# SSD decays in a hybrid trunk kernel: running sums sent through a DRAM scratch instead of selected inputs and matmuls

## The chip, the cores and the metric

The kernel runs on one core of one Trainium2 chip. The core has five engines that work side by side and wait for one another through semaphores. TensorE (PE in the profile) multiplies matrices, and its weight loads are listed apart as PEld. VectorE (DVE) does elementwise work, ScalarE (ACT) activations and copies, GpSimd (POOL) more elementwise work and selects, SyncE (SP) issues the DMA transfers. A DMA queue is worked off by sixteen DMA engines. SBUF is the working memory, PSUM holds what TensorE writes, DRAM is the large memory outside.

The metric is the device time of one execution in microseconds (us), lower is better. Three timed runs of the kernel before gave 1427.46, 1426.99 and 1427.30 us, median 1427.3.

## The reference

The reference is a trunk of two layers over 512 tokens of width 1024. Layer 0 is a Mamba-2 (SSD) mixer followed by a squared-ReLU MLP, layer 1 a stick-breaking attention followed by another MLP. A LayerNorm of `alpha * h + sublayer(h)` stands after each of the four. The change touches only the SSD mixer, and in it the decays:

```
a_cs      = cumsum(a)                                   # a = dt * -exp(a_log), per head
decay_mat = exp(segsum(a))                              # exp(a_cs[l] - a_cs[s]) for s <= l, else 0
cb        = einsum("bclgn,bcsgn->bcgls", cc, bc)        # C_l . B_s, one per group
y_diag    = einsum("bcgls,bcgrls,bcsgrp->bclgrp", cb, decay_mat, xc)
states    = einsum("bclgn,bcgrl,bclgrp->bcgrpn", bc, exp(a_cs[-1] - a_cs), xc)
prev      = scan: carry * exp(a_cs[-1]) + states        # from chunk to chunk
y_off     = einsum("bclgn,bcgrpn,bcgrl->bclgrp", cc, prev, exp(a_cs))
y         = rmsnorm_per_group((y_diag + y_off + D * x) * silu(z)) * norm_w @ w_out
```

There are 32 heads in 8 groups of 4. The sums over a chunk don't depend on where chunks are cut, and the kernel uses four chunks of 128 tokens where the reference uses eight of 64.

## The kernel before

Products are made in split precision: each operand is a rounded part (`hi`, `h`) plus a remainder (`lo`, `l`), and `mm3` (L206) issues three matmuls for one product. A weight tile is fetched by `emit_w` (L149): SP loads `wr`, ACT casts it to `wh` (L190), DVE or, for every fourth tile, POOL subtracts to get `wl` (L192). There are two buffers for `wr` and four for `wh`/`wl`, so SP waits for an older tile's split before it fetches the next.

`ssm` (L565) is the SSD layer. It loads the transposed input `xf` in five pieces, splits it into `x_h` and `x_l`, and then runs:

- `time_steps` (L617): the time-step projection `pdt` (24 matmuls), a transpose `pdtt`, a chain of some twenty small operations on 128x128 tiles for the softplus (L628 to L640), `da` (L644) and its split `da_h`, `da_l` (L645, L646). Then four small matmuls make the running sums `pa` (tile `pacs`) with the triangle `tri_le`, and the totals `pt_` (tile `ptot`) with ones. From these come `E`, `bdec` and `dec_s`.
- for each group g: `in_bc` and `in_x` (projections `pB`, `pC`, `px`, convolution and SiLU), `in_z` (`pz`), `in_xt` (transposes `pxt`, the tiles `xd`, `xe`, `dx`), `decays`, `scores` (C.B into `cbm`), and for each chunk c `front` (the product of decay and score, split into `W`, and the state carry `prev`) and `back` (`po`, `py`). Then `gate` and `finish` (`pyt`). After groups 3 and 7 `tok_out` multiplies by the output weights (`so`).

`decays(q)` (L762) makes the decay tiles of a group before. For each of the four chunks POOL copies `da_h` and `da_l` of four heads over 128 columns with the triangle cut out (two affine_selects of 128x512, tiles `dm`, one buffer each), PE multiplies both by `tri_gt` into a PSUM tile `sg` (two matmuls of 128x512), and ACT takes one exponential of 128x512 into `dec`. The upper triangle of `dec` is 1 there, and the select on `cbm` (L788) puts zeros in. In `front`, `dec` is multiplied by `cbm` on DVE, and on POOL for chunk 3.

What sets the order: a scheduler with a timeline model places each engine's instructions when the program is built; each engine then works through its own list strictly in order. Tiles of one tag share a fixed number of buffers. PSUM has two tags of four buffers, `mm` (`pdt`, `pB`, `pC`, `px`, `pz`, `so`) and `bg` (the small tiles and `sg`). `table_order` (L661) keeps the SiLUs and the exponentials of ACT in batches, since changing between them costs a table load.

Of the kernel before, what the change touches and what calls it, by code (L numbers as in the profile page):

```python
# [11 lines left out]
F32 = mybir.dt.float32  # L12
F32R = mybir.dt.float32r
AF = mybir.ActivationFunctionType
ALU = mybir.AluOpType
# [20 lines left out]
def trunk(ctx: ExitStack, tc: tile.TileContext, io):  # L36
# [6 lines left out]
    ps = ctx.enter_context(tc.tile_pool(name="ps", bufs=4, space=PSUM))  # L43

# [9 lines left out]
    def f(x):  # L54
        return x.bitcast(F32)
# [11 lines left out]
    for _ in range(14):  # L67
# [497 lines left out]
    def ssm(sp, nxt_ln):  # L565
# [38 lines left out]
        def small(name, dt=F32):  # L604
            return sp.tile(CH, dt, name=name)
# [9 lines left out]
        dec_s = small("dec_s")  # L615

        def time_steps():  # L617
# [31 lines left out]
            for o, l in ((pa, tri_le), (pt_, ones_r)):  # L649
                nc.tensor.matmul(o, l, da_h, start=True, stop=False)  # L650
                nc.tensor.matmul(o, l, da_l, start=False, stop=True)
            nc.scalar.activation(E, pa, AF.Exp)
# [109 lines left out]
        def decays(q, cs=range(NT)):  # L762
            g = q.g
            hs = slice(4 * g, 4 * g + 4)
            if cs[0] == 0:
                q.dec = []
            for c in cs:
                nm = f"{g}_{c}"
                dm = pair(f"dm{nm}", S4, "dm", 1)
                for o, i in zip(dm, (da_h, da_l)):  # L770
                    nc.gpsimd.affine_select(o, f(i[:, c, hs]).unsqueeze(2).to_broadcast(S4), pattern=[[0, 4], [1, P]],
                                            compare_op=ALU.is_ge, fill=0.0, base=0, channel_multiplier=-1)
                pseg = psum("bg", S4, f"sg{nm}")
                nc.tensor.matmul(pseg, tri_gt, dm[0], start=True, stop=False)
                nc.tensor.matmul(pseg, tri_gt, dm[1], start=False, stop=True)
                dec = sp.tile(S4, F32, tag="dec", name=f"dec{nm}", bufs=4)
                table_order("exp", nc.scalar.activation(dec, pseg, AF.Exp))
                q.dec.append(dec)

        def scores(q):  # L780
            g = q.g
            pcb = psum("bg", [P, NT, P], f"cb{g}")
            for c in range(NT):
                cs = slice(c * P, (c + 1) * P)
                mm3(pcb[:, c, :], (q.B[0][:, cs], q.B[1][:, cs]), (q.C[0][:, cs], q.C[1][:, cs]), True, True)
            q.cbm = sp.tile([P, NT, P], F32, tag="cbm", name=f"cbm{g}", bufs=1)
            nc.scalar.copy(q.cbm, pcb)
            nc.gpsimd.affine_select(q.cbm, q.cbm, pattern=[[0, NT], [1, P]], compare_op=ALU.is_ge, fill=0.0,  # L788
                                    base=0, channel_multiplier=-1)
            q.pr = [None] * NT  # L790
            q.W = [None] * NT

        def front(q, c):
# [4 lines left out]
            eng = nc.gpsimd if c == 3 else nc.vector  # L798
            eng.tensor_tensor(dec, dec, q.cbm[:, c, :].unsqueeze(1).to_broadcast(S4), op=ALU.mult)
# [81 lines left out]
        run(in_x(cur, 1))  # L881
        decays(cur)
        in_xt(cur)
        v = None
        for g in range(G):
# [15 lines left out]
            front(q, 1)  # L901
# [3 lines left out]
            front(q, 2)  # L905
# [3 lines left out]
            front(q, 3)  # L909
# [22 lines left out]
            if g % 4 == 3:  # L932
# [5 lines left out]
                else:  # L938
                    nxt_ln.load_rows(lambda j, c0: sp.tile(S4, F32, tag="dec", name=f"lnr{j}{c0}", bufs=4)
# [340 lines left out]
```

## Time and profile before

| | before |
|---|---|
| median of three timed runs | 1427.3 us |
| profiled execution, its own time | 1426.79 us |
| span of that execution | 1424.7 us |
| mean granted TensorE clock | 0.994 |
| busy, share of the span: PE / PEld | 98% / 84% |
| busy: DVE / ACT / POOL | 76% / 55% / 16% |
| moved by DMA | 162.99 MB, mean 114 GB/s |

Busy time of PE counts matmuls from start to a modelled end, and one starts before the one ahead has ended. What a matmul costs a full PE is therefore the distance from its start to the next start, not its own duration. Granted clock is the share of TensorE's full clock that the hardware allowed in a stretch. The SSD layer is the first 450 us or so of the span; the two MLPs and the attention follow.

### The profile page before, as it was taken

What the parts mean: (1) busy time and instruction counts of PE and PEld (TensorE: products, weight loads), DVE (VectorE), ACT (ScalarE), POOL (GpSimd) and SP (SyncE); (2) the same over time, 40 slices, a digit from 0 to 9 for tenths busy, and PEclk for the clock granted to TensorE, in tenths of its full rate; (3) what the DMA queues carried; (4) which work ended last, traced back from release to release, by engine and by line L of the source; (5) the groups of instructions that cost most, each with busy time, mean ns of one, the idle gap of its engine ahead of it and who ended that gap; (6) DMA issues with size and microseconds to landing.
All of it is one profiled execution on the core that took longest, in us unless ns stands there. A gap on an engine that the chain in (4) does not pass through costs nothing. (4 is left out here: it accounts for less than half of the span.)

```text
span 1424.7 us, 19323 instructions
## 1 busy us (share of the span) xinstructions
PE 1394.1 (98%) x7414; PEld 1199.9 (84%) x7414; DVE 1078.2 (76%) x1530; ACT 783.9 (55%) x1264; POOL 221.4 (16%) x249
## 2 busy tenths in 40 slices
PE   9999999999999999999999899999999999999996
PEld 6898897889997988888888789899878888888885
DVE  5798898368877695876849868787867876858587
ACT  5556574246653453626345468898842735454453
POOL 2344555135443100000000200000000000000001
PEclk9999999999999999999999999999999999999999
DMA  5223212221223356455443421121223455454533
GB/s 185 75 77 131 75 60 75 89 89 60 75 75 104 125 157 179 132 179 161 148 148 120 146 89 38 52 75 45 89 75 118 131 165 162 149 175 136 176 111 126
DMA packets 46699, 162.99 MB, mean 114 GB/s; under 512 B 5520, under 2 KB 5776, under 8 KB 46608
## 3 DMA queue, kind: packets, MB, share of 16 engines
q1 hardware_dynamic: 44016, 157.44, 35.4%
q10 hardware_dynamic: 2592, 4.33, 1.0%
q8 instruction: 58, 0.95, 0.3%
q14 instruction: 33, 0.27, 0.1%
HBM read 159.65 MB, written 2.10 MB: 114 GB/s over the span
## 5 line engine op out<-in xcount | busy, mean ns | idle before, releaser
L190 ACT CAST wh<-wr 128x1024 fp32r<-128x1024 f32 x235 | 246.7, 1050 | 328.5 <-DMA wr<-w 165.1
L192 DVE TENSOR_TENSOR wl<-wr,wh 128x1024 fp32r<-128x1024 f32 x218 | 268.4, 1232 | 184.3 <-ACT wh L190 182.9
L208 PE MATMUL f<-ln_hl,wh 128*128 128x512 f32 (+1 forms) x544 | 201.2, 371 | 0.0
L209 PE MATMUL f<-ln_hh,wl 128*128 128x512 f32 (+1 forms) x544 | 201.1, 370 | 0.0
L207 PE MATMUL f<-ln_hh,wh 128*128 128x512 f32 (+1 forms) x544 | 200.4, 371 | 0.0
L208 PEld LDWEIGHTS f<-ln_hl,wh 128*128 128x128 f32 x544 | 102.3, 188 | 17.6 <-DVE ln_hl L399 0.2
L209 PEld LDWEIGHTS f<-ln_hh,wl 128*128 128x128 f32 x544 | 102.3, 188 | 17.4
L207 PEld LDWEIGHTS f<-ln_hh,wh 128*128 128x128 f32 x544 | 101.9, 188 | 17.5
L347 POOL TENSOR_TENSOR ln_rs<-ln_sums 128x1 f32<-128x1 f32 (+1 forms) x6 | 3.1, 523 | 635.3 <-ACT lnr L345 635.3
L208 PE MATMUL X<-wl,hP 128*128 128x512 f32 x192 | 74.7, 389 | 0.0
L207 PE MATMUL X<-wh,hP 128*128 128x512 f32 x192 | 74.7, 389 | 0.0
L209 PE MATMUL X<-wh,l 128*128 128x512 f32 x192 | 74.2, 390 | 0.2 <-DVE l L460 0.2
L209 PE MATMUL pz<-wh,x_l 128*128 128x256 f32 x256 | 72.8, 284 | 0.0
L208 PE MATMUL pz<-wl,x_h 128*128 128x256 f32 x256 | 72.6, 284 | 0.0
L207 PE MATMUL pz<-wh,x_h 128*128 128x256 f32 x256 | 72.5, 283 | 0.0
L459 ACT CAST hP<-r 128x512 fp32r<-128x512 f32 x80 | 48.1, 620 | 32.4 <-DVE r L471 31.5
L192 POOL TENSOR_TENSOR wl<-wr,wh 128x1024 fp32r<-128x1024 f32 x17 | 42.5, 2503 | 93.3 <-ACT wh L190 92.9
L207 PE MATMUL px<-x_h,wh 128*128 128x512 f32 x128 | 50.8, 397 | 0.0
L208 PE MATMUL px<-x_l,wh 128*128 128x512 f32 x128 | 50.2, 393 | 0.0
L209 PE MATMUL px<-x_h,wl 128*128 128x512 f32 x128 | 50.2, 392 | 0.0
L208 PE MATMUL Y<-wl,hP 128*128 128x512 f32 x128 | 49.8, 389 | 0.0
L208 PEld LDWEIGHTS pz<-wl,x_h 128*128 128x128 f32 x256 | 48.7, 190 | 0.9
(1365 smaller groups left out, 3930.7 us busy)
## 6 DMA issues: line engine op xcount, KB each, us to landing
wr<-w SPq DMA_DIRECT2D x160, 512.0 KB, 3.6
wr<-w_bc SPq DMA_DIRECT2D x16, 512.0 KB, 3.6
wr<-w_x SPq DMA_DIRECT2D x16, 512.0 KB, 3.6
wr<-w_z SPq DMA_DIRECT2D x16, 512.0 KB, 3.5
wr<-w_so SPq DMA_DIRECT2D x16, 512.0 KB, 3.6
rawa<-w SPq DMA_DIRECT2D x16, 512.0 KB, 3.6
rawc<-w SPq DMA_DIRECT2D x16, 512.0 KB, 4.5
wr<-w_qk SPq DMA_DIRECT2D x16, 512.0 KB, 3.6
```

Source lines behind the costliest of these rows:

```text
L190: nc.scalar.copy(hi, raw)
L192: eng.tensor_sub(lo, raw, f(hi))
L207: nc.tensor.matmul(out, a[0], b[0], start=start, stop=False, skip_group_check=skip)
L208: nc.tensor.matmul(out, a[0], b[1], start=False, stop=False, skip_group_check=skip)
L209: return nc.tensor.matmul(out, a[1], b[0], start=False, stop=stop, skip_group_check=skip)
L347: nc.gpsimd.tensor_add(rs, self.sq[:, t0:t1, 0], self.sq[:, t0:t1, 1])
L459: nc.scalar.copy(h, src)
```

## The change

The decay of a chunk is exp(a_cs[l] - a_cs[s]) for s <= l. The tile has s on the partitions and l along the columns. After the change a_cs[l] is brought to all 128 partitions by DMA, and a_cs[s], which is one number per partition, enters as the bias of the exponential:

- `time_steps` makes the running sums a second time, transposed (`pcsr`, two matmuls of 128x128, a PSUM tile of tag `mm`), copies them to SBUF (`csr`) and writes them to a DRAM tile `cs_rows`; a scaled copy of `pa` gives the negative sums `ncs`.
- `spread(q, c)` loads the four rows of a group and chunk from DRAM to all partitions (256 KB, queue of SP) and puts -1e30 above the diagonal with one affine_select in place on POOL. The four spreads of a group are called in `front` of the group ahead, one per chunk. `dec` has six buffers instead of four.
- `decays(q)` is 16 exponentials of 128x128 with a bias each, in place.
- the `dm` selects, the `sg` matmuls, `tri_gt` and the select on `cbm` are gone; `front` multiplies on DVE for every chunk.

```diff
+    dp = ctx.enter_context(tc.tile_pool(name="dp", bufs=1, space=bass.MemoryType.DRAM))
...
-    tri_gt = cp.tile([P, P], F32R, name="tri_gt")
-    nc.gpsimd.affine_select(tri_gt, one, pattern=[[-1, P]], compare_op=ALU.is_gt, fill=0.0,
-                            base=0, channel_multiplier=1)
...
+        ncs = small("ncs")
+        cs_rows = dp.tile([NT, H, P], F32, name="cs_rows")
...
             for o, l in ((pa, tri_le), (pt_, ones_r)):
                 nc.tensor.matmul(o, l, da_h, start=True, stop=False)
                 nc.tensor.matmul(o, l, da_l, start=False, stop=True)
+            pr = psum("mm", [P, P], "pcsr")
+            for i, x in enumerate((da_h, da_l)):
+                nc.tensor.matmul(pr, x.rearrange("p c h -> p (c h)"), tri_le, start=i == 0, stop=i == 1)
+            rows = sp.tile([P, P], F32, name="csr")
+            nc.scalar.copy(rows, pr)
+            nc.sync.dma_start(cs_rows.rearrange("c h t -> (c h) t"), rows)
+            nc.scalar.activation(ncs, pa, AF.Copy, scale=-1.0)
...
-        def decays(q, cs=range(NT)):
+        def spread(q, c):
             g = q.g
-            hs = slice(4 * g, 4 * g + 4)
-            if cs[0] == 0:
+            if c == 0:
                 q.dec = []
-            for c in cs:
-                nm = f"{g}_{c}"
-                dm = pair(f"dm{nm}", S4, "dm", 1)
-                for o, i in zip(dm, (da_h, da_l)):
-                    nc.gpsimd.affine_select(o, f(i[:, c, hs]).unsqueeze(2).to_broadcast(S4), pattern=[[0, 4], [1, P]],
-                                            compare_op=ALU.is_ge, fill=0.0, base=0, channel_multiplier=-1)
-                pseg = psum("bg", S4, f"sg{nm}")
-                nc.tensor.matmul(pseg, tri_gt, dm[0], start=True, stop=False)
-                nc.tensor.matmul(pseg, tri_gt, dm[1], start=False, stop=True)
-                dec = sp.tile(S4, F32, tag="dec", name=f"dec{nm}", bufs=4)
-                table_order("exp", nc.scalar.activation(dec, pseg, AF.Exp))
-                q.dec.append(dec)
+            dec = sp.tile(S4, F32, tag="dec", name=f"dec{g}_{c}", bufs=6)
+            nc.sync.dma_start(dec.rearrange("p h t -> p (h t)"),
+                              cs_rows[c, 4 * g:4 * g + 4, :].rearrange("h t -> (h t)").partition_broadcast(P))
+            nc.gpsimd.affine_select(dec, dec, pattern=[[0, 4], [1, P]], compare_op=ALU.is_ge, fill=-1e30,
+                                    base=0, channel_multiplier=-1)
+            q.dec.append(dec)
+
+        def decays(q):
+            for c, dec in enumerate(q.dec):
+                for h in range(4):
+                    i = 4 * q.g + h
+                    table_order("exp", nc.scalar.activation(dec[:, h, :], dec[:, h, :], AF.Exp,
+                                                            bias=ncs[:, c, i:i + 1]))
...
             nc.scalar.copy(q.cbm, pcb)
-            nc.gpsimd.affine_select(q.cbm, q.cbm, pattern=[[0, NT], [1, P]], compare_op=ALU.is_ge, fill=0.0,
-                                    base=0, channel_multiplier=-1)
...
-            eng = nc.gpsimd if c == 3 else nc.vector
-            eng.tensor_tensor(dec, dec, q.cbm[:, c, :].unsqueeze(1).to_broadcast(S4), op=ALU.mult)
+            nc.vector.tensor_tensor(dec, dec, q.cbm[:, c, :].unsqueeze(1).to_broadcast(S4), op=ALU.mult)
...
         run(in_x(cur, 1))
+        for c in range(NT):
+            spread(cur, c)
         decays(cur)
...
+            def first(c):
+                front(q, c)
+                if nxt:
+                    spread(nxt, c)
+
             scores(q)
             fill.run(4)
-            front(q, 0)
+            first(0)
```

(The other three calls of `front` become `first` in the same way.)

The scheduler places the work anew. First place, the start of the program on PE. `pdt` is the time-step projection, `pB` the first projection of group 0, `pacs`, `ptot` and `pcsr` the running sums, totals and transposed sums. Before, right behind the warm-up:

```order
L207 MATMUL pdt<-x_h,wdthi 128x512
L208 MATMUL pdt<-x_l,wdthi 128x512
L209 MATMUL pdt<-x_h,wdtlo 128x512
L207 MATMUL pB_241<-x_h,wh_129 128x512
L208 MATMUL pB_241<-x_l,wh_129 128x512
L207 MATMUL pdt<-x_h,wdthi 128x512
L209 MATMUL pB_241<-x_h,wl_130 128x512
L207 MATMUL pB_241<-x_h,wh_129 128x512
```

After the change, the end of the 24 `pdt` matmuls, which now stand together, and what follows:

```order
L207 MATMUL pdt<-x_h,wdtlo 128x512
L625 MATMUL pdtt<-ident,dT 128x128 x4
L650 MATMUL pacs<-da_h,tri_le 128x128
L650 MATMUL ptot<-da_h,ones_r 128x128
L654 MATMUL pcsr<-tri_le,da_h 128x128
L205 MATMUL pB_250<-x_h,wh_129 128x512
L206 MATMUL pB_250<-x_l,wh_129 128x512
```

Before, `pB` was woven into `pdt`, `pC` and `px` stood next, and `pacs` came far behind, after the 24 matmuls each of `pB`, `pC` and of the next group's `pB`, 48 of `px` and 23 of the next `pC`. Now no `pB` matmul stands ahead of the first `pcsr` matmul, which reads `da_h`. `pcsr` was written as a tile of the same PSUM tag as `pB`, and ahead of it in the program.

Second place, the same stretch on DVE, which makes `da_h` from `pdtt` (`dtt` are its temporaries, `ca_B` and `ca_C` the convolutions, `wl` weight remainders). Before:

```order
L628 TENSOR_TENSOR dtt_201<-pdtt,hv 128x128
L672 SCALAR_TENSOR_TENSOR ca_C_315<-pC_290,cw,ca_C_315 128x509
L694 CAST B0h<-ca_B_266 128x512
L639 TENSOR_SCALAR dtt_201<-dtt_201 128x128
L631 TENSOR_SCALAR dtt_201<-dtt_201 128x128
L695 TENSOR_TENSOR B0l<-ca_B_266,B0h 128x512
L632 RECIPROCAL dtt_201<-dtt_201 128x128
L694 CAST C0h<-ca_C_315 128x512
```

After the change:

```order
L628 TENSOR_TENSOR dtt_203<-pdtt,hv 128x128
L190 TENSOR_TENSOR wl_296<-wr_293,wh_295 128x1024
L639 TENSOR_SCALAR dtt_203<-dtt_203 128x128
L631 TENSOR_SCALAR dtt_203<-dtt_203 128x128
L632 RECIPROCAL dtt_203<-dtt_203 128x128
L633 TENSOR_TENSOR dtt_203<-dtt_203 128x128
L634 TENSOR_TENSOR dtt_203<-dtt_203 128x128
L635 TENSOR_SCALAR dtt_203<-dtt_203 128x128
L637 SCALAR_TENSOR_TENSOR dtt_203<-dtt_203 128x128 x6
L638 SCALAR_TENSOR_TENSOR dtt_203<-dtt_203 128x128
L640 SCALAR_TENSOR_TENSOR dt<-dtt_203 128x128
L644 SCALAR_TENSOR_TENSOR dtt_204<-dt,dtt_204 128x128
```

The chain stands in one piece now, with one weight remainder (of the second `px` weight tile) behind its first step; the convolutions have moved behind it.

Third place, group 1, on POOL and on SP. `pv` is the state carry of group 1, `dec` a spread tile of group 2 or 3, `yg` the output accumulation. POOL before:

```order
L788 AFFINE_SELECT cbm_990<-cbm_990 128x512
L799 TENSOR_TENSOR dec_3_955<-dec_3_955,cbm_990 128x512
L192 TENSOR_TENSOR wl_1359<-wr_1356,wh_1358 128x1024
L810 TENSOR_TENSOR pv_0_1021<-pv_0_1021,bdec 128x256 x2
L841 TENSOR_TENSOR yg_1097<-yl_0_1108,dx_886 128x256
```

POOL after the change:

```order
L190 TENSOR_TENSOR wl_1386<-wr_1383,wh_1385 128x1024
L814 TENSOR_TENSOR pv_0_1028<-pv_0_1028,bdec 128x256
L776 AFFINE_SELECT dec_2_1180<-dec_2_1180 128x512
L814 TENSOR_TENSOR pv_0_1028<-pv_0_1028,bdec 128x256
L776 AFFINE_SELECT dec_3_1263<-dec_3_1263 128x512
L845 TENSOR_TENSOR yg_1114<-yl_0_1125,dx_914 128x256
```

SP after the change, the loads that these selects wait for (before, the same weights stood there without the `dec` rows):

```order
L164 DMA wr_1509<-w_z 128x1024
L947 DMA v<-x 128x4x1024
L164 DMA wr_1578<-w_z 128x1024
L774 DMA dec_2_1180<-cs_rows 128x512
L774 DMA dec_3_1263<-cs_rows 128x512
L164 DMA wr_1656<-w_x 128x1024
```

A select that waits for a load now stands between the two carry multiplies of a group, and that load stands behind a weight load on SP.

More of the change, by code (lines that the diff above doesn't have):

```diff
@@ L904, in ssm @@
             fill.run(4)
-            front(q, 2)
+            first(2)
             fill.run(4)
@@ L908, in ssm @@
             fill.run(4)
-            front(q, 3)
+            first(3)
             fill.run(4)
@@ L938, in ssm @@
                 else:
-                    nxt_ln.load_rows(lambda j, c0: sp.tile(S4, F32, tag="dec", name=f"lnr{j}{c0}", bufs=4)
+                    nxt_ln.load_rows(lambda j, c0: sp.tile(S4, F32, tag="dec", name=f"lnr{j}{c0}", bufs=6)
                                      .rearrange("p a c -> p (a c)"), T)
```

2 lines of the change are left out of this document (1 added, 1 removed).

## The prediction

> **What bounds the kernel now.** I read the page's totals first, then the busy times by stretch, then the waits of PE.
>
> ```profile
> PE 1394.1 (98%) x7414; PEld 1199.9 (84%) x7414; DVE 1078.2 (76%) x1530; ACT 783.9 (55%) x1264; POOL 221.4 (16%) x249
> 50.00:200.00 150.00, 148.06 (x961) 133.99 (x961) 131.88 (x209) 94.00 (x170) 74.85 (x78) 1.00 0.27 87
> 250.00:400.00 150.00, 150.00 (x910) 133.87 (x909) 106.13 (x167) 77.43 (x134) 54.49 (x56) 1.00 0.26 78
> PE pyt L864 <- DVE yg L859: 1.4, 1, 1.4
> PE st L207 <- ACT dec L777: 1.0, 1, 1.0
> ```
>
> In both stretches of the SSD layer (the columns are the stretch and its length, then busy us of PE, PEld, DVE, ACT and POOL) PE is busy for all but 2 of 300 us; DVE has 88% and 71%, ACT 63% and 52%. The last two rows are the two longest waits of PE inside the groups, 2.4 us together, against some 400 us of them. So PE bounds the groups: a matmul removed there shortens them by what it took from the stream, and work put on ACT or DVE costs nothing as long as their gaps hold it.
>
> **What is removed from PE.** The `sg` matmuls are listed in eight groups of eight, 64 in all; first and last group, then two places in the stream:
>
> ```profile
> L774 PE MATMUL sg<-dm_0h,tri_gt x8: 393/476/481, 49.1 to 399.3; 128*128 128x512 f32 x8
> L775 PE MATMUL sg<-dm_3l,tri_gt x8: 389/477/485, 60.4 to 413.1; 128*128 128x512 f32 x8
> ```
>
> ```profile
> 98.26 0.40 PE L774 MATMUL sg<-dm_1h,tri_gt 128*128 128x512 f32 x1
> 98.50 0.28 PE L208 MATMUL pz<-wl,x_h 128*128 128x256 f32 x1
> 98.96 0.40 PE L775 MATMUL sg<-dm_1l,tri_gt 128*128 128x512 f32 x1
> 99.19 0.28 PE L209 MATMUL pz<-wh,x_l 128*128 128x256 f32 x1
> ```
>
> They last 0.39 to 0.48 us but overlap. From start to next start they take 0.24 and 0.23 us. 64 x 0.235 = **15.0 us** leave PE. (By duration it would be some 26 us, which the stream never spent.)
>
> **What is added at the start.** The order of the changed kernel puts all of `pdt`, `pdtt`, `pacs`, `ptot` and the first `pcsr` ahead of the first `pB`. PE works through its list in order, so it now waits for the whole softplus chain with nothing else to do. Before, PE had `px` and more to run while that chain went on, from 29.55 us to the first `pacs` at 48.39. I rebuild the chain from its rows of before:
>
> ```profile
> 14.11 3.91 DVE L590 TENSOR_TENSOR x_l<-xf,x_h 128x512 fp32r<-128x512 f32 x4 [2.95 <-ACT x_h L589]
> 23.43 0.58 ACT L622 COPY dT<-pdt 128x512 f32<-128x512 f32 x1
> 28.41 0.60 PE L625 MATMUL pdtt<-ident,dT 128*128 128x128 f32 x4
> 29.55 0.28 DVE L628 TENSOR_TENSOR dtt<-pdtt,hv 128x128 f32<-128x128 f32 x1
> 9.38 6.63 SPq L166 DMA_DIRECT2D wr<-w_x  x2
> wr<-w_x SPq DMA_DIRECT2D x16, 512.0 KB, 3.6
> 23.91 1.05 ACT L190 CAST wh<-wr 128x1024 fp32r<-128x1024 f32 x1
> 25.00 1.22 DVE L192 TENSOR_TENSOR wl<-wr,wh 128x1024 fp32r<-128x1024 f32 x1 [0.20 <-ACT wh L190]
> 34.37 0.94 DVE L632 RECIPROCAL dtt<-dtt 128x128 f32<-128x128 f32 x1
> 45.00 0.28 DVE L638 SCALAR_TENSOR_TENSOR dtt<-dtt 128x128 f32<-128x128 f32 x1
> 45.32 0.29 DVE L640 SCALAR_TENSOR_TENSOR dt<-dtt 128x128 f32<-128x128 f32 x1
> 26.36 0.39 PE L207 MATMUL px<-x_h,wh 128*128 128x512 f32 x1
> 48.39 0.22 PE L650 MATMUL pacs<-da_h,tri_le 128*128 128x128 f32 x1
> 48.79 0.51 PE L702 MATMUL pbt<-ident,ca_B 128*128 128x128 f32 x3
> ```
>
> The input arrives by the same DMAs, and ACT and DVE split it in the same order, so its last remainder ends at 14.11 + 3.91 = 18.0 us again. Two `pdt` matmuls stand behind it: the last ends by 18.7. The copy `dT` (0.58) gives 19.3, the transposes (0.60) 19.9, the first step on DVE (0.28) 20.2. Now DVE has the weight remainder in its way: SP issued that weight at 9.38 + 6.63 = 16.0, it lands 3.6 later, 19.6; its cast (1.05) ends at 20.7, its remainder (1.22) at 21.9. The two activations of the chain on ACT fit in beside it. From there DVE runs the chain alone: a step depends on the one before and starts 0.32 after it (45.00 to 45.32). Two products, six polynomial steps and the three behind them are 11 x 0.32 = 3.5; the reciprocal is 0.94; four small operations, the cast `da_h` among them, I take at 0.22 each, 0.9. The chain ends at 21.9 + 5.3 = 27.2 us. From the end of the transposes at 19.9 until then PE stands still, 7.3 us.
>
> Then come the two trios of running sums; four such matmuls took 48.79 - 48.39 = 0.4, so six take 0.6. `pB` and `pC` are 48 matmuls at 0.23, 11.0. `px` would begin at 27.2 + 0.6 + 11.0 = 38.8, where it began at 26.36 before. Before still had the transposes (0.35 to the next start) and the small sums (0.4) ahead of it, so PE is behind by 38.8 - 26.4 - 0.75 = **11.6 us**.
>
> **The clock after the hole.** Where PE has little to do in this trace, its clock falls:
>
> ```profile
> 1052.54 0.78 PE L1139 MATMUL o<-w712h,vp 128*128 128x512 f32 x1 [1.18 <-ACT w712h L1126]
> 1054.28 0.63 PE L208 MATMUL al<-wl,o_h 128*128 128x512 f32 x1
> 1054.71 0.63 PE L209 MATMUL al<-wh,o_l 128*128 128x512 f32 x1
> 1055.99 0.40 PE L209 MATMUL al<-wh,o_l 128*128 128x512 f32 x1
> 804.00:805.00 1.00, 0.00 (x0) 0.50 0.84 340
> 809.00:810.00 1.00, 1.00 (x6) 0.50 0.00 0
> ```
>
> After short waits around 1050 us the starts are 0.43 apart (1054.28 to 1054.71) instead of 0.23, and a matmul lasts 0.63 us, until 0.40 is back at 1055.99: from 1052.54 on 3.4 us at half rate, which lose 1.7. The last two rows (the number behind the busy time is the granted clock) show 0.50 over a gap of 2.5 us at 805 and still at 810, 4.5 us after work resumed there: 2.3 lost. A hole of 7.3 us should cost at least the smaller, so I take **1.7 us**; the bounds are 0 and 2.3.
>
> TensorE: Matmul & The Clock Gate (the Trainium skill, Part 1, What's actually happening) says that an idle window of about 3.4 us halves the clock and that as long a busy stretch restores it: by that the price would also be 1.7 us, once. The trace goes further than the page, since at 1052 it halves after waits of about a microsecond; by the trace the thin `pdt` stretch, 24 matmuls spread over 12 us, could be halved too, which would add some 0.4 us behind the last input and make the sum 0.4 worse than by the page.
>
> **What lies beside PE.** The rows from which the rest is priced:
>
> ```profile
> L777 ACT ACTIVATE dec<-sg 128x512 f32<-128x512 f32 x32 | 19.0, 596 | 14.0 <-PE sg L775 13.9
> 50.99 0.28 ACT L652 ACTIVATE E<-pacs 128x128 f32<-128x128 f32 x1
> L799 DVE TENSOR_TENSOR dec<-dec,cbm 128x512 f32<-128x512 f32 x24 | 23.5, 1028 | 1.0 <-POOL cbm L788 1.0
> L788 POOL TENSOR_SCALAR_AFFINE_SELECT cbm<-cbm 128x512 f32<-128x512 f32 x8 | 5.6, 695 | 32.4 <-ACT cbm L787 32.4
> lnr<-lnrow ACTq DMA_DIRECT2D x12, 256.0 KB, 3.6
> xf<-xT SPq DMA_DIRECT2D x3, 512.0 KB, 6.5
> 122.33 0.61 POOL L810 TENSOR_TENSOR pv<-pv,bdec 128x256 f32<-128x256 f32 x1 [3.08 <-DVE pr_1l L816]
> 116.71 0.34 SPq L166 DMA_DIRECT2D wr<-w_z  x1
> ```
>
> ACT: 128 biased exponentials of 128x128 at up to 0.28 (nearest row, also 128x128) are 36 us against 19.0, 2 us more per group, where ACT has 16 us of gaps in 44. POOL loses 64 selects, the eight `cbm` selects and eight products, and gains 32 selects of some 0.7. DVE gets the eight products, 1.0 us each, one per group, against 5 us of gaps in 44. All three at nothing; if the cover of DVE were gone, at 88% the tightest, they would cost 8 us, and the exponentials at most their 17.
>
> The way through DRAM: the write of 64 KB and the broadcast loads have no row of their own. The nearest, broadcast loads of 256 KB, land in 3.6 us; a load among several takes 6.5. For group 0 two such steps lie between the copy `csr` (about 33 us) and the exponentials, which also wait for the SiLU of the second `px`, not before 50: hidden between 3.6 and 6.5 alike. In later groups the loads stand on SP among the weights, and a select on POOL can make the second carry multiply wait. In group 1 SP could issue the load at about 117.1, behind the weight of 116.71; it lands at 120.7, the select ends at 121.4, and the carry started at 122.33. So it fits with 0.9 us to spare: nothing in the forecast. Loads of 6.5 us would miss by 2.0 in each of seven groups, 14 us: the upper bound.
>
> **The sum**, against the profiled execution's own 1426.8 us (0.5 under the median): -15.0 (`sg`) + 11.6 (hole) + 1.7 (clock) = -1.7, so **1425.1 us**. On the median it is 0.15% less. This measurement can tell about 0.2%, 2.9 us, from no change, so the likeliest case is "same", close to the edge.
>
> **Rivals.**
> - The hole costs less. Without the clock's fall it is 1.7 less; and the two waits of PE on `dec` and `yg` (2.4) may go, since POOL is relieved, and the `bg` PSUM tiles no longer carry `sg`: 1425.1 - 1.7 - 2.4 = 1421.0. For it speaks that during the hole weights and convolutions get ahead of PE; against it that PE hardly waited for them before.
> - The loads come late (slower). The place is the select between the two carries; it decides from a landing of 3.6 + 0.9 = 4.5 us. At 5.5 us each of seven groups loses 1.0, and PE waits at `po`: 1432. For it speaks that the queue of SP now holds 33 more transfers, some behind a weight that waits for a buffer; against it the low DMA share, 0.27.
> - PE's hole isn't there, because PE is not held by the list as I read it: 1426.8 - 15.0 = 1412. Against it stands the order itself, `pcsr` ahead of `pB`, which reads `da_h`.
>
> **How the numbers follow.** Forecast (1422.5 to 1428.5) 0.52, of which a third lies below 1424.4, the bound for faster; cheaper hole 0.24; late loads 0.17; no hole 0.07. Faster: 0.17 + 0.24 + 0.07 = 0.48. Slower: most of the late loads, 0.15. Same: 0.37. The range goes from 1417 to 1432: it holds the forecast, the cheaper hole and the nearer half of the late loads, and leaves the full 1412 and the far end of the loads out.
>
> **What would show it.** Right: PE idle from about 20 to 27 us, released by DVE `da_h`; granted clock 0.5 in part of that stretch and for some 3 us behind it; `px` first at about 39 to 41; the groups' period shorter by 1.8 us each; no `sg`. Wrong: PE waits in the groups on `po`, `st` or `py` of over 1 us each (late loads or a slow ACT), SP waits ahead of `dec` loads with weights landing late, or `pB` running before 25 us.

## The result, and the profile after

The changed kernel takes 1440.07 us (median of 4, 1439.40 to 1440.91), the kernel before 1427.38 beside it: ratio 1.0092, 95% interval 1.008 to 1.0104. It is 12.7 us slower; the prediction said 1425.1.

The page of the changed kernel, its totals, and below them PE's busy tenths and granted clock in 40 slices of 36 us:

```profile
PE 1390.6 (97%) x7352; PEld 1195.4 (83%) x7352; DVE 1067.6 (74%) x1538; ACT 800.7 (56%) x1360; POOL 174.8 (12%) x200
...
PE   6999998999999999999999899999999999999996
...
PEclk7999999899999999999999999999999999999999
```

PE's total is 3.5 us smaller and the span 13.2 longer (1437.9): PE stands still for longer. Two slices lack clock, the first and the eighth (252 to 288 us). PE's starts around these places in the timeline:

```profile
22.17 0.63 PE L625 MATMUL pdtt<-ident,dT 128*128 128x128 f32 x4 [0.77 <-ACT dT L622]
...
29.77 0.45 PE L650 MATMUL pacs<-da_h,tri_le 128*128 128x128 f32 x1 [6.98 <-DVE da_h L645]
...
43.84 0.39 PE L205 MATMUL px<-x_h,wh 128*128 128x512 f32 x1
...
250.77 0.66 PE L868 MATMUL pyt<-ident,yg 128*128 128x128 f32 x2 [5.81 <-DVE yg L863]
```

And two stretches of its windows view (PE's busy time stands first behind the length, the granted clock behind the five busy times):

```profile
12.00:20.50 8.50, 5.93 (x14) 3.84 (x13) 5.01 (x5) 4.37 (x6) 2.35 (x1) 0.50 0.48 162
...
250.80:256.00 5.20, 5.11 (x23) 4.71 (x23) 3.08 (x7) 1.26 (x3) 0.00 (x0) 0.50 0.33 101
```

The first hole is the one that was forecast: 6.98 us of waiting for `da_h`. The clock is at half twice here: from 11 to 21 us, while `pdt` runs, and, after 3.4 us at full, again from 24.6 us in the hole to 34.85, 5.1 us after work resumed. `px` begins at 43.84 (before 26.36, forecast 40.5). The second hole was not forecast: in front of the first `pyt` of group 3, at the output projection `so`, PE waits 5.8 us, and the clock then stays at half for 9.3 us. In the kernel before, that `pyt` came without a wait:

```profile
236.54 0.38 PE L864 MATMUL pyt<-ident,yg 128*128 128x128 f32 x2
```

What releases it is the finish of group 3. ACT and DVE of the changed kernel, in order:

```profile
233.20 1.28 ACT L784 ACT_TABLE_LOAD   x1
234.50 4.21 ACT L784 ACTIVATE dec<-dec,ncs 128x128 f32<-128x128 f32 x14
238.62 0.40 ACT L852 ACTIVATE sz<-yg 128x256 f32<-128x256 f32 x1
239.01 0.35 ACT L844 COPY yl<-py 128x256 f32<-128x256 f32 x1
...
243.57 2.86 DVE L741 TENSOR_TENSOR xd<-xt,xd 128x512 fp32r<-128x512 f32 x1
246.36 0.41 DVE L846 TENSOR_TENSOR yg<-py,yg 128x256 f32<-128x256 f32 x1
250.27 1.14 DVE L863 TENSOR_SCALAR yg<-yg,ss 128x256 f32<-128x256 f32 x4 [1.19 <-POOL ss L861]
```

ACT does 14 exponentials of group 4 in one burst ahead of three of the four squares of group 3's gate (`sz`) and of two of its copies `yl`. Not all of the wait need be theirs: the last addition to `yg` on DVE (246.36) also stood behind an `xd` of 2.86 us, where the `xd` ahead of it took 1.24. In the kernel before, the last squares of the gate came ahead of all four exponentials, each of which reads its own `sg`, and the four stood apart:

```profile
217.23 0.42 ACT L848 ACTIVATE sz<-yg 128x256 f32<-128x256 f32 x1
...
218.62 0.41 ACT L848 ACTIVATE sz<-yg 128x256 f32<-128x256 f32 x1
...
226.17 0.60 ACT L777 ACTIVATE dec<-sg 128x512 f32<-128x512 f32 x1
227.66 0.60 ACT L777 ACTIVATE dec<-sg 128x512 f32<-128x512 f32 x1 [0.90 <-PE sg L775]
232.86 0.59 ACT L777 ACTIVATE dec<-sg 128x512 f32<-128x512 f32 x1
239.46 0.59 ACT L777 ACTIVATE dec<-sg 128x512 f32<-128x512 f32 x1
```

### The profile page after: what moved, and what is told of

It reads as the page before. It is cut to its first block, busy times and chain, and to the rows that moved or that the text cites. A ratio compares the mean times of both kernels' runs of the same rounds, so it can differ in the third digit from the quotient of the medians.

```text
span 1437.9 us, 19309 instructions
## 1 busy us (share of the span) xinstructions
PE 1390.6 (97%) x7352; PEld 1195.4 (83%) x7352; DVE 1067.6 (74%) x1538; ACT 800.7 (56%) x1360; POOL 174.8 (12%) x200
## 5 line engine op out<-in xcount | busy, mean ns | idle before, releaser
L205 PE MATMUL Y<-wh,hP 128*128 128x512 f32 x128 | 49.3, 389 | 0.0
```

What stands on the lines that cost most here:

```text
L205: nc.tensor.matmul(out, a[0], b[0], start=start, stop=False, skip_group_check=skip)
```

## The experiments

Differences in us are against the kernel before in the same series (1426.4 to 1427.4), and where two other kernels are compared, it is these differences that are; the ratio stands with its interval. An order edge (`after_` in the diffs: the first instruction stands behind the second on its engine) adds no semaphore.

### The hole at the start

**Hole alone**, added to the kernel before:

```diff
+            pr = psum("mm", [P, P], "pcsr")
+            for i, x in enumerate((da_h, da_l)):
+                nc.tensor.matmul(pr, x.rearrange("p c h -> p (c h)"), tri_le, start=i == 0, stop=i == 1)
+            rows = sp.tile([P, P], F32, name="csr")
+            nc.scalar.copy(rows, pr)
```

> The kernel before, with one thing of the change added: the matmul pcsr of da_h and da_l in a PSUM tile of tag mm, and its copy csr. The sg matmuls, the selects and the 128x512 exponentials stay as before; nothing goes through DRAM. PE's list then reads pdt, pdtt, pacs, ptot, pcsr, pB, as in the changed kernel. Theory A (the lag of 16.8 us at the first px of the changed kernel is the hole with its slow clock, and it stays to the end): 1427.4 + 16.8 = 1444, at least 1441, the prediction's own 13.3. Between the last py3 and the first pyt of group 3 stand 99 matmuls here, as many as before (98), so no wait there. Rival B (the lag of the start is made up later in the groups, and the 13 us of the change come from the loads and the exponentials): 1427 to 1431.

1442.29, ratio 1.0104 (1.0089 to 1.0119): +15.3. Theory A holds. PE waits 6.98 us for `da_h` here too, `px` begins at 43.41, and of its lag of 17.05 us there 16.1 are left at the first `f` of the MLP.

**Clock held up in the hole**, 38 matmuls whose output nobody reads, in the changed kernel:

```diff
+            def dummy(n, other):
+                for _ in range(n):
+                    after_(nc.tensor.matmul(dum, ones_r, ones_r.unsqueeze(1).to_broadcast([P, 4, P]),
+                                            start=True, stop=True), other)
...
+                dummy(2 if 2 <= k < 7 else 0, m)
...
+            dummy(28, m)
```

> The changed kernel, with 38 extra matmuls whose output nobody reads: two behind each of the third to the seventh pdt step, and 28 behind pdtt, in the time in which PE waits for da_h. Nothing else changes its place. Theory A (of the lag of 16.8 us, 11.6 are the wait and the order, as forecast, and the rest is the clock, at half rate from about 12 to 34 us): the granted clock stays up, pdt ends some 2 us earlier, pB and pC run 0.23 apart from the start, and the time falls from 1440.1 by about 5, to 1434 to 1437. Rival (the wait alone makes the lag, and its length was underestimated): 1439 to 1441.

1438.52, ratio 1.0073 (1.0055 to 1.0092). In its trace PE starts:

```profile
28.82 0.30 PE L670 MATMUL pacs<-da_h,tri_le 128*128 128x128 f32 x1
40.50 0.39 PE L212 MATMUL px<-x_h,wh 128*128 128x512 f32 x1
```

`px` is 3.3 us earlier than in the changed kernel (43.84). The clock is at 1.00 from 14.7 us on; only from 11.3 to 14.7 was it at half here too. So 3.3 us is what nearly all of the slow clock costs, in this one profile. The time fell by 1.2, less than the 3 to 6 expected, and the two intervals overlap; the trace shows the size, the times alone don't.

**Sums in tag bg**, one word changed:

```diff
-            pr = psum("mm", [P, P], "pcsr")
+            pr = psum("bg", [P, P], "pcsr")
```

> The changed kernel with pcsr in a PSUM tile of tag bg in place of mm; nothing else is edited. pB and pC are then woven into the pdt matmuls as in the kernel before, and pacs and pcsr stand in the px stretch. Theory A: the start gains the 16.7 us of the first hole, 1423; but all later fill slips ahead as well, and only 27 matmuls in place of 56 are left between the last py3 and the first pyt of group 3, so the second hole may grow by up to 29 x 0.23 = 6.7 us: 1422 to 1431. Rival B (loads and exponentials make the loss): 1437 to 1441.

1424.24, ratio 0.9981 (0.9972 to 0.9991): the first hole is gone, `px` begins at 26.83, and the kernel is 15.4 us faster than the changed one. The second hole is still there and larger:

```profile
237.24 0.66 PE L868 MATMUL pyt<-ident,yg 128*128 128x128 f32 x2 [6.87 <-DVE yg L863]
```

### The second hole: order edges on ACT and PE

**Exponentials behind the gate**: those of group 4 are held behind the last square of group 3's gate.

```diff
+                    if q.g == 4:
+                        after_(a, gated[0])
```

> The changed kernel with one order edge more: the 16 exponentials of group 4 stand behind the last square of group 3's gate on ACT; PE's list is the same as in the changed kernel up to a few matmuls. Theory A (the second hole, 6.2 us in front of the first pyt of group 3 with about 4 us of slow clock behind it, is released late because ACT runs 4.2 us of exponentials ahead of that gate): the wait at pyt falls to about 2 us or less and the time to 1432 to 1436. Rival B (the finish of group 3 is late from other work, the DVE and POOL steps of the next group, or PE simply has too few matmuls left there): the wait stays at 5 us or more, 1438 to 1441.

1437.09, ratio 1.0068 (1.0051 to 1.0084). The wait of 5.8 us at `pyt` is gone, as Theory A said, but the time fell by only 2.6, for a new wait took its place, at the products of group 4 that now stand behind the burst:

```profile
246.38 0.38 PE L883 MATMUL pyt<-ident,yg 128*128 128x128 f32 x2
249.77 0.38 PE L212 MATMUL st<-xe4h,bt4h 128*128 128x256 f32 x1 [1.09 <-ACT xe4h L757]
252.23 0.58 PE L215 MATMUL st<-xe4l,bt4h 128*128 128x256 f32 x1 [2.08 <-DVE xe4l L758]
```

**Both edges** (also the second `px` half of group 4 behind the second `py` of group 3), then the same **with tag bg**:

```diff
+            if (g, j) == (4, 1):
+                hold[:] = last_py
...
+        if hold:
+            after_(m, hold.pop())
```

> The changed kernel with two order edges: the first px matmul of group 4's second half behind the last py of group 3's second chunk on PE, and the 16 exponentials of group 4 behind the last square of group 3's gate on ACT. PE's list then has 68 so matmuls of the first output half between the first pyt of group 3 and the scores of group 4, where the changed kernel has two matmuls. Theory A (the second hole is a finish made late by ACT with too little left for PE to do, and the wait on xe that took its place in the run with one edge comes from the same shortage): no wait over 1.5 us in front of pyt or st, the jump of the lag at so falls from 7 to 8 us to under 1.5, time 1431 to 1435. Rival C (the work on DVE and ACT at this place takes that long in any order, and the wait only moves on): a wait of 3 us or more at cb, st or py of group 4, 1436 to 1438.

> pcsr in a PSUM tile of tag bg and the two order edges together. Theory A (two holes, each with its own cause, the matmuls of sg saved on top): from 1424.2 of the run with bg alone by another 7 to 8, 1414 to 1418, which is the kernel before less the 15.0 us of sg plus 3 to 4 of small waits. Rival C (the wait moves on): 1421 to 1425.

1437.42, ratio 1.0078 (1.0062 to 1.0094), and 1424.29, ratio 0.9979 (0.9970 to 0.9989): no gain over one edge, and none over tag bg alone. Rival C is right: the wait moves on. With tag bg it stands at `W` of group 3:

```profile
206.80 0.47 PE L856 MATMUL py<-xd,W_0h 128*128 128x128 f32 x1 [2.88 <-ACT W_0h L820]
209.55 0.42 PE L857 MATMUL py<-xd,W_0l 128*128 128x64 f32 x1 [1.52 <-DVE W_0l L821]
```

So the hole is not one unlucky instruction; the chain of a group as a whole is late by then. Theory A had the place, not the cause.

### The loads

Each broadcast load issued twice, and none at all:

```diff
             nc.sync.dma_start(dec.rearrange("p h t -> p (h t)"),
                               cs_rows[c, 4 * g:4 * g + 4, :].rearrange("h t -> (h t)").partition_broadcast(P))
+            nc.sync.dma_start(dec.rearrange("p h t -> p (h t)"),
+                              cs_rows[c, 4 * g:4 * g + 4, :].rearrange("h t -> (h t)").partition_broadcast(P))
```

```diff
-            nc.sync.dma_start(dec.rearrange("p h t -> p (h t)"),
-                              cs_rows[c, 4 * g:4 * g + 4, :].rearrange("h t -> (h t)").partition_broadcast(P))
-            nc.gpsimd.affine_select(dec, dec, pattern=[[0, 4], [1, P]], compare_op=ALU.is_ge, fill=-1e30,
+            nc.gpsimd.affine_select(dec, low.unsqueeze(1).to_broadcast(S4), pattern=[[0, 4], [1, P]], compare_op=ALU.is_ge, fill=-1e30,
```

> The changed kernel with every broadcast load of the running sums from DRAM issued twice into the same tile, the second behind the first, 32 more transfers on SP; the selects wait for the second. The order of PE moves a little in group 3: 64 matmuls in place of 56 between its last py and the first pyt. Theory A (the loads are hidden, the loss is the two holes): 1437 to 1442, and the lag falls through groups 0 to 3 as in the changed kernel, by 7 to 9 us. Rival D (the late loads of the prediction: each us of landing later costs a us per group): the second load adds 2 us or more to each landing, seven groups, 1450 or more, or at least 1445.

> The changed kernel with the 32 broadcast loads left out: the selects read a tile filled once with a large negative constant, so the decays come out as zero and the output is not the reference's. The write of the sums stays, and so do the selects and the exponentials. The order of PE moves a little: 64 matmuls in place of 56 between the last py and the first pyt of group 3. Theory A: 1437 to 1441. Rival D (late loads): faster by 5 or more, 1435 or less, with the gain spread over groups 1 to 7.

Twice: 1451.70, ratio 1.0176 (1.016 to 1.0193), 12.0 us above the changed kernel, the size that Rival D gave. None: 1436.71, ratio 1.0076 (1.0059 to 1.0093), which overlaps with the changed kernel's interval. In the one profile without loads `px` began at 39.88, 4.0 us earlier than in the changed kernel, with the granted clock at 1.00 between 13 and 18 us where that had 0.50; from `px` to the end of the span it gained 0.9. So the loads as they are (landing in 3.7 us, median) cost at most some 3 us, but they have little room.

### The exponentials

**Wide exponentials with tag bg**, one per chunk, the bias left out:

```diff
-                for h in range(4):
-                    i = 4 * q.g + h
-                    table_order("exp", nc.scalar.activation(dec[:, h, :], dec[:, h, :], AF.Exp,
-                                                            bias=ncs[:, c, i:i + 1]))
+                table_order("exp", nc.scalar.activation(dec, dec, AF.Exp))
```

> pcsr in a PSUM tile of tag bg, and one exponential of 128x512 per chunk in place of four of 128x128 with a bias; the bias (the running sum at the source position) is left out of the computation, so the output is not the reference's. The loads, the selects and everything else stay. Theory E (the 16 exponentials of a group stand on ACT between the last SiLU of the next group and its products, and between the squares of the gate and the finish; this chain, not PE, sets the pace of the groups once sg is gone; PE hides it by taking the next group's matmuls ahead, and pays at so, where none are left): the scores of group 3 stand ahead of the pz matmuls again on PE's list, no wait over 2 us at pyt, lag falls to about -7 us before so and does not jump back by more than 2: 1415 to 1418. Rival F (the loads, or the products given to DVE, are as much to blame): the wait of 5 us or more stays, 1422 to 1425.

1411.99, ratio 0.9897 (0.9882 to 0.9913): -15.2, 12.5 better than tag bg alone. That is Theory E, and below its range; Rival F falls. The exponentials of group 4 and the `pyt` behind them, first with tag bg alone, then with wide ones:

```profile
217.17 3.92 ACT L784 ACTIVATE dec<-dec,ncs 128x128 f32<-128x128 f32 x13
```

```profile
220.12 2.19 ACT L782 ACTIVATE dec<-dec 128x512 f32<-128x512 f32 x4
224.55 0.70 PE L865 MATMUL pyt<-ident,yg 128*128 128x128 f32 x4 [0.98 <-DVE yg L860]
```

Narrow ones start 0.30 us apart, so 16 take 4.8 us in a group; four wide ones take 2.2. Where the time went shows in the starts of PE at this boundary:

| | first `cb` of group 3 | first `so` | last `py` of group 3 | its first `pyt` | first `f` of the MLP |
|---|---|---|---|---|---|
| before | 193.92 | 217.69 | 215.23 | 236.54 | 469.59 |
| changed | 210.88 | 223.72 | 234.67 | 250.77 | 482.13 |
| tag bg | 200.13 | 207.86 | 227.34 | 237.24 | 467.43 |
| tag bg, wide | 183.10 | 208.75 | 213.49 | 224.55 | 453.88 |

With tag bg alone PE reaches `so` as early as with wide exponentials, by doing the next group's `px` and its own `pz` ahead of the scores `cb`: 7.7 us lie between `cb` and `so`, with wide ones 25.7. The finish of group 3 then has too little left beside it. In the groups PE's busy time mostly hides this; it shows where the next group's work has been used up.

The windows view settles what became of the saving. Three stretches: from the first `px` to the first `f` of the MLP with tag bg alone, the slow clock in it around the second hole, and the stretch from `px` to `f` with wide exponentials (PE's busy time stands first behind the length):

```profile
26.83:467.43 440.60, 428.44 (x2547) 378.42 (x2545) 336.42 (x565) 260.15 (x518) 137.67 (x140) 0.98 0.32 103
234.82:245.06 10.24, 7.68 (x29) 6.93 (x30) 8.08 (x18) 4.21 (x8) 1.81 (x2) 0.50 0.17 51
26.56:453.88 427.32, 421.81 (x2548) 373.68 (x2546) 334.77 (x565) 240.26 (x422) 140.63 (x140) 1.00 0.33 106
```

The length less the busy time is PE's idle time. At granted clock 0.50 the starts are 0.43 apart instead of 0.23, so an estimated 0.47 of the busy time there is lost. The same for five traces, in us:

| | first `px` to first `f` | PE idle | lost at half clock | the rest: PE's work |
|---|---|---|---|---|
| before | 443.2 | 6.5 | 0 | 436.7 |
| changed | 438.3 | 11.8 | 4.1 | 422.4 |
| tag bg | 440.6 | 12.2 | 5.2 | 423.2 |
| tag bg, wide | 427.3 | 5.5 | 0 | 421.8 |
| before, without `sg` (below) | 435.6 | 9.7 | 1.6 | 424.3 |

Without `sg` PE's work is 12 to 15 us shorter in every row: that saving arrives. With narrow exponentials it is paid back, 6.7 us in waits and 5.2 in slow clock behind them (tag bg against tag bg, wide).

**In the changed kernel itself**, with its hole at the start (same edit):

> The changed kernel (pcsr in tag mm, so with the hole at the start) with one exponential of 128x512 per chunk in place of four of 128x128 with a bias; the bias is left out of the computation, so the output is not the reference's. Theory E, the two causes adding up: 1412.0 + 15.3 of the hole alone = 1427, 1425 to 1430. If the wide exponentials gain only where there is no hole at the start: 1436 or more.

1428.26, ratio 1.0012 (1.0002 to 1.0021), 10.8 less than the changed kernel. The two causes add up.

**In the kernel before**, without a bias, and then with a bias column of zeros:

```diff
-                table_order("exp", nc.scalar.activation(dec, pseg, AF.Exp))
+                for h in range(4):
+                    table_order("exp", nc.scalar.activation(dec[:, h, :], pseg[:, h, :], AF.Exp, bias=zb[:, c, i:i + 1]))
```

> The kernel before, with each 128x512 exponential split into four of 128x128, without bias; nothing else of the change. Theory E (the narrow exponentials cost only where the matmuls of sg no longer cover the chain of the groups; here PE still has them, and 82 matmuls stand between the last py and the first pyt of group 3): 1427 to 1431. Rival H (the narrow exponentials cost their 12 us in any surroundings): 1437 or more.

> The kernel before, with each 128x512 exponential split into four of 128x128 that take their bias from a column of an SBUF tile, as in the changed kernel; the column holds zeros. In the run with narrow exponentials and no bias four of them took 0.79 us in place of 0.60, so that run added only 0.8 us a group; with a bias they should take 1.2, as in the changed kernel, 2.4 a group more. Theory E (they cost only once the sg matmuls are gone): 1426 to 1430. Rival H (they cost their 12 us in any surroundings): 1436 or more.

1424.48, ratio 0.9988 (0.9978 to 0.9997), and 1431.39, ratio 1.0033 (1.0021 to 1.0044). Four without a bias took 0.79 us, so the first was a weak test. At 1.15 us for four they cost 4.4 us, all in groups 6 and 7: the first `cb` of group 6 still starts 2.3 us earlier than in the kernel before, that of group 7 starts 1.9 later and the first `f` of the MLP 5.2 later. Neither theory's number: it is a third of the 12.

**Narrow without a bias, tag bg**:

```diff
-                    table_order("exp", nc.scalar.activation(dec[:, h, :], dec[:, h, :], AF.Exp,
-                                                            bias=ncs[:, c, i:i + 1]))
+                    table_order("exp", nc.scalar.activation(dec[:, h, :], dec[:, h, :], AF.Exp))
```

> pcsr in a PSUM tile of tag bg, the 16 exponentials of a group kept at 128x128, but without the bias, so the output is not the reference's. It lies between the run with biased narrow exponentials (1424.2) and the run with wide ones (1412.0). Theory E (the time that ACT needs for them sets the loss): if four take 0.8 us without the bias, a third of the extra ACT time is left, 1414 to 1418. Rival I (their number, or the order that the scheduler gives 16 in place of 4, makes the loss): 1422 to 1425.

1430.58, ratio 1.0029 (1.0018 to 1.0041): above both expectations and 6.4 slower than with the bias, though 16 took some 3.3 us in place of 4.8. Length on ACT alone does not set the loss; the scheduler's order differs as well.

**The order on PE alone**, with tag bg: `pz` held behind the last matmul of its group's scores (`q.cb`), ACT unchanged.

```diff
+                            if k == 0:
+                                hold[:] = q.cb
```

> pcsr in a PSUM tile of tag bg, the 16 biased exponentials of a group as in the changed kernel, and one order edge per group: pz, the group's own gate projection, which the list of PE has taken ahead of the group's scores, is held behind them. PE's list then has 149 or more matmuls of fill behind the scores of each group, as in the run with wide exponentials (where 121 and more stand there), against none to 70 in the run with bag bg alone. Everything on ACT keeps its length. Theory J (the loss is in the order on PE: the fill of a group is used up ahead of its scores, and at so nothing is left): 1412 to 1417. Theory E (the length of the exponentials on ACT itself sets the pace): PE now waits for the chain in each group, at cb, pyt or py, 1423 or more.

1449.47, ratio 1.0155 (1.0126 to 1.0184), 25.4 above tag bg alone. Without the work taken ahead, PE waits for the finish of the groups, 22 us in three waits:

```profile
PE pyt L879 <- DVE yg L874: 22.0, 3, 9.4
```

Theory J's number did not come, but the run doesn't decide against it. The edge takes `pz` away from beside the finish of the group ahead, and the same edge costs nearly as much with wide exponentials (the last run, below). What it shows is that the chain from `py` over the gate to `pyt` is longer than the work that is then left beside it. How the 12 us divide between the length of the exponentials and the order that the scheduler writes for sixteen of them stays open.

### The matmuls of sg alone

The kernel before without them; the exponentials read the masked operand:

```diff
-                nc.tensor.matmul(pseg, tri_gt, dm[0], start=True, stop=False)
-                nc.tensor.matmul(pseg, tri_gt, dm[1], start=False, stop=True)
-                table_order("exp", nc.scalar.activation(dec, pseg, AF.Exp))
+                table_order("exp", nc.scalar.activation(dec, f(dm[1]), AF.Exp))
```

> The kernel before without the 64 sg matmuls, and nothing of the change added: the exponentials (128x512, as before) read the masked operand in SBUF, so the decays and the output are not the reference's. Theory E and the prediction's own term say that sg is worth its 64 x 0.235 = 15.0 us where the chain of the groups stays as it was: 1411 to 1414. Rival G (the chain of the groups has no room at all, whatever the exponentials: any matmul removed there is paid back at so): half of the 15 us at most, 1419 or more.

1418.84, ratio 0.9941 (0.9927 to 0.9956): -8.4, between the two. So `sg` alone gives half of its 15 us: by the table above PE's work shrinks by 12.4, but it idles 3.2 more and loses 1.6 at half clock. The chain of the groups has little room. One thing is not separated here: the exponentials now read `dm`, of which there is one buffer, so POOL's next select also waits for ACT. With the change's other parts and wide exponentials it is 15.2. Those parts also take selects and products from POOL; they were not tried one by one.

### Versions that compute all of it with wide exponentials

The source's sum subtracted on POOL; and a load that adds to a tile in which the select has put that negative sum:

```diff
+            nc.gpsimd.tensor_tensor(dec, dec, ncs[:, c, 4 * g:4 * g + 4].unsqueeze(2).to_broadcast(S4), op=ALU.add)
```

```diff
+            nc.gpsimd.affine_select(dec, ncs[:, c, 4 * g:4 * g + 4].unsqueeze(2).to_broadcast(S4),
+                                    pattern=[[0, 4], [1, P]], compare_op=ALU.is_ge, fill=-1e30,
+                                    base=0, channel_multiplier=-1)
+            nc.gpsimd.dma_start(dec.rearrange("p h t -> p (h t)"),
+                              cs_rows[c, 4 * g:4 * g + 4, :].rearrange("h t -> (h t)").partition_broadcast(P),
+                              accum_op=ALU.add)
```

> A version that computes all of it: pcsr in tag bg, the running sum at the source position subtracted on POOL, by one 128x512 operation with a broadcast operand per chunk behind the load, then the select, then one exponential of 128x512 without bias. Theory E: near the run with wide exponentials, with POOL's 32 extra operations in the gaps of an engine that is busy 12%: 1415 to 1420. Rival (POOL's queue, with waits for loads ahead of its additions for yg, makes the finish of the groups late): 1423 or more, with waits of PE at pyt, pxt or po on yg.

> A version that computes all of it with wide exponentials: the select comes first and writes the negative running sum of the source position under the mask, then the broadcast load adds the running sums to it on the way in (an accumulating DMA, issued by POOL), then one exponential of 128x512 per chunk; pcsr in tag bg. Theory E (narrow exponentials on ACT are what took the pace from PE): 1411 to 1417, as the run with wide exponentials. Rival (32 transfers issued by POOL hold its queue and make the additions for yg late, as the subtraction on POOL did): 1423 or more, with waits of PE on yg.

On POOL: 1433.44, ratio 1.0036 (1.0023 to 1.0048), with waits on `yg` as the rival said. Accumulating load: **1420.54**, ratio 0.9957 (0.9943 to 0.9972), between the two expectations. It beats both kernels, the changed one by 1.3% (by the two ratios to the kernel before). With `pz` held as above it loses that:

> The version with accumulating loads and wide exponentials (1420.5, computes all of it) with the same order edge per group: pz behind the scores. Theory J: 1411 to 1416. Theory E, or POOL's issue of 32 transfers as the limit: 1419 to 1423.

1443.91, ratio 1.0120 (1.0105 to 1.0135), 22.9 above the version without the edge. PE waits 16.1 us at `pyt` in four waits, so the edge itself makes them, with wide exponentials too.

## Why the prediction was wrong

- **sg, -15.0.** The price per matmul was right: PE's work behind the first `px` is 14.3 us shorter in the changed kernel. That PE bounds the groups was right only as they stood: without `sg` the chain beside PE takes over, and alone the removal gives -8.4.
- **The hole, +11.6.** The mechanism and the place were right: 6.98 us of idle time against 7.3, released by `da_h`. The size was short: with the clock held up `px` began at 40.50, where 38.8 was forecast, since the chain started later (the last `pdt` ended at 20.2 there and at 21.4 in the changed kernel, where 18.7 was forecast).
- **The clock, +1.7.** Mis-sized: 3.3 in the trace, outside the bounds 0 to 2.3. The half rate began in the thin `pdt` stretch, which was mentioned and priced at 0.4, and the two stretches together cost twice the term. Hole and clock measured 15.3 (alone) to 17.1 (with wide exponentials), against 13.3. The page that was cited, TensorE: Matmul & The Clock Gate (the Trainium skill, Part 1, What's actually happening), has an idle window of about 3.4 us before the clock falls; here it fell at 10.95 us though PE was busy for 1.81 of the 3.41 us ahead of that, and stayed at 0.50 from 12 to 20.5 us with PE 70% busy, so the trace goes further. That a second hole would slow the clock again, 4.1 us by the table, was not in the sum.
- **"All three at nothing" is the step that failed.** The exponentials were covered by "16 us of gaps in 44" on ACT. A sum of gaps says nothing about a chain: the burst stands between the last SiLU of the next group and its products, and ahead of the gate and finish of the group. Their cost is 10.8 to 12.5 us, paid as waits of PE for the chain and as half clock behind them, inside the bound of 17 that the text gave and then didn't use for a rival. How much of it is their length and how much the order of sixteen is open, as said.
- **Rivals.** Late loads were priced from a landing of 4.5 us on; they land in 3.7, and the loss came by another way. The cheaper hole did not come. That the expected gain is paid back at the output projection was not among the rivals, and the order was read at three places, none of them at `so`.

By runs the change's 12.7 us are -8.4 (`sg` alone), -6.8 (its other parts, wide exponentials, no hole), +17.1 (the hole) and +10.8 (narrow exponentials). Taken in another order the steps would come out a little differently: the hole is 15.3 on the kernel before.

## What to carry to other kernels

An engine that is 98% busy may be so because the order lets it work ahead; take work from it, and the chain beside it can become the bound, with most of the bill where nothing is left to take ahead. So price work that is added to a "free" engine by the chain it lengthens, and look at the end of each layer or stage. A tile of a shared PSUM tag, allocated early and fed late, can put the work allocated behind it in that tag behind it in the list: here one word (`mm` to `bg`) was worth 15 us.

## What the runs showed of the hardware

- The clock came back late: 5.1 us after work resumed at 29.77 (starts 0.43 apart until 34.82, then 0.26 and 0.23), and 9.3 us after 250.77, with one wait of 0.56 us in between; from the changed kernel's trace:

```profile
34.82 0.42 PE L206 MATMUL pB<-x_l,wh 128*128 128x512 f32 x1
35.08 0.39 PE L207 MATMUL pB<-x_h,wl 128*128 128x512 f32 x1
...
259.63 0.63 PE L206 MATMUL so<-wl,yT0h 128*128 128x512 f32 x1
260.06 0.43 PE L207 MATMUL so<-wh,yT0l 128*128 128x512 f32 x1
```

- The clock changes in steps of 3.41 us. All three stretches at half in the SSD layer of the changed kernel last 10.24 us, and the full one between the first two 3.42; in the other traces stretches at half there last 3.41, 6.83, 10.24, 13.65 or 20.48. So the bill of a wait jumps: the wait of 5.8 us was followed by 9.3 us at half.

```profile
10.95:21.19 10.24, 7.67 (x18) 4.83 (x16) 5.23 (x6) 4.37 (x6) 2.35 (x1) 0.50 0.54 183
21.19:24.61 3.42, 0.84 (x5) 0.42 (x4) 1.75 (x5) 2.28 (x5) 0.00 (x0) 1.00 0.26 104
24.61:34.85 10.24, 5.08 (x14) 4.14 (x15) 4.86 (x15) 0.00 (x0) 0.00 (x0) 0.50 0.16 51
249.89:260.13 10.24, 8.80 (x32) 7.65 (x33) 7.74 (x15) 3.28 (x6) 0.96 (x2) 0.50 0.17 51
```

- A bias column makes a 128x128 exponential longer. Tile views (minimum, median and maximum in ns) with the bias (the run with tag bg) and without it (the run of narrow ones without a bias), both from SBUF:

```profile
L784 ACT ACTIVATE dec<-dec,ncs x128: 384/387/404, 58.4 to 407.9; 128x128 f32<-128x128 f32 x128
```

```profile
L784 ACT ACTIVATE dec<-dec x128: 293/294/314, 58.1 to 404.6; 128x128 f32<-128x128 f32 x128
```

- An accumulating broadcast load of 256 KB, issued by POOL, takes 0.91 us of POOL and lands after 5.2 us, against 3.7 us for the plain load from SP.
